# The first layer norm's sum is centred ahead of the last two parts of the output product, and the norm's steps are regrouped

## The chip, the cores and the metric

The kernel runs on one core of a Trainium2 chip. Its metric is the device time of one execution in microseconds (us); of several executions the median counts. A core has TensorE (PE in the profile, with PEld for its weight loads), VectorE (DVE), ScalarE (ACT), GpSimd (POOL) and SyncE (SP, which issues most of the transfers), each with a queue of its own that is worked off in order. They share the on-chip memory SBUF (128 partitions); PE writes its products to PSUM, from where DVE or ACT fetch them.

## The reference

One inference step of a decoder with two layers. 512 prompt positions and 8 x 8 sample positions, 576 columns in all, go through the same weights. The first layer has a mixer of two head groups, an RWKV-7 recurrence and a retention; their outputs are joined and multiplied by one output matrix. The second layer has a short convolution. Behind each mixer there is an MLP, and behind all four of them a layer norm over the 1024 features:

```python
def layer_norm(x, g, b):
    xf = x.astype(jnp.float32)
    mu = jnp.mean(xf, -1, keepdims=True)
    var = jnp.mean(jnp.square(xf - mu), -1, keepdims=True)
    return ((xf - mu) * lax.rsqrt(var + LN_EPS)).astype(x.dtype) * g + b
...
        x = layer_norm(ALPHA * x + y, ln1_g[l], ln1_b[l])
        x = layer_norm(ALPHA * x + sqrelu_mlp(x, w_up[l], w_down[l]), ln2_g[l], ln2_b[l])
```

with `y = concat([ya, yb]) @ w_out` in the first layer, and `sqrelu_mlp` the square of relu(x @ w_up), times w_down. The change is about the first of these norms, and about the order of the work ahead of it.

## The kernel before

Everything lies feature-major: a matrix of 1024 features by 576 columns is eight tiles of 128 x 576, and each tile is worked on in two halves of 288 columns, g=0 and g=1. A tile's statistics over the features are sums over partitions and tiles, which PE makes with a matrix of constants. Products of full accuracy are made in three matmuls: each operand is split into a high part `hi` (a cast on ACT, L77) and the rest `lo` (a subtraction on DVE, L78), and `mm3` multiplies hi by hi, lo by hi and hi by lo (L152, L153, L154).

*The mixer stage* ends at about 497 us. Twelve Python generators issue it: the input projection (`projs`), the preparation of the four head pairs of the recurrence (`pres`, `stages`, `back` 0 to 3 with the chained scans `ch` and the outputs `po`), the sample columns, the retention's front and back for four pairs, and `wout`, the output product. The function `drive` calls them in turn, and the order in which it does so, with the priority it sets, decides the order on the engines. Before the change `drive` reads this order from the table `SCHEDULE`, 424 pairs of a generator's number and a priority, worked out beforehand.

*The output product* (`Wout`) is added up in parts, as its inputs are finished (`WP`): part 0 multiplies the blocks k=0, 1, 2 of the joined heads, part 1 k=3, 4, 5, and part 2 k=6. Part 0 waits for recurrence pair 2 (`ya2`), part 1 for pair 3 (`ya3`) and the retention pairs 0 and 1, and part 2 for retention pair 2. For each of the eight output tiles m a part loads a piece of the weights (`wr`, two buffers), splits it on ACT (L1306) and POOL (L1307), multiplies into the PSUM tiles `wa`, and adds to x on DVE: L1336 in part 0, L1338 in parts 1 and 2. The weights for k=7 are loaded and split ahead of time (`keep`, after part 0). Their products (`acc<-hh,kh`) stand in the next stage, in front of the norm.

*The first norm* is fed one tile after the other by `ln_add`. On the first tile it makes an estimate of the mean from that tile alone (`cps`, L246), which seven subtractions on POOL and one on DVE take off all eight tiles (L255), so that squares stay small. Then each tile gets its last addition (L257), its sum `ps` (L283), its square on ACT (L260) and the square's sum `pq` (L283). `ln_finish` makes mean and variance, the reciprocal root by Ln and Exp on ACT with one Newton step on DVE (L294 to L302), and for each tile x - mean on DVE (L309), times the root on POOL or DVE (L310), and times gamma plus beta on ACT (L313). A split into hi and lo follows (L77, L78). All of it is done for g=0 and for g=1.

*The first MLP* begins with the head: four output tiles in ordinary products (`acc<-he`, `acc<-ho`), each with a Relu on ACT (L1588), a square on DVE (L1589, `evac_up`) and a split. Beside them POOL makes sums and differences of x (`ts`, L1564), which the products behind the head use (`acc<-ht`, function `gemm7`), in a scheme of seven products in place of eight. The second MLP, in the second layer, begins in the same way.

## Time and profile before

| quantity | value |
|---|---|
| time, median of 3 | 1573.41 us (1572.03 to 1576.05) |
| time of the profiled execution | 1570.47 us |
| its span | 1568.7 us |
| PE, DVE, ACT, POOL busy | 94%, 69%, 41%, 36% |
| last product of the input projection | 353.5 us |
| last x addition of part 0 | 437.6 us |
| last x addition of part 1 | 479.0 us |
| last x addition of part 2 | 497.0 us |
| first product of the first MLP | 523.1 us |
| first product behind its head | 571.5 us |

The span is the time from the first to the last recorded instruction; the profiled execution's own time is 1.8 us longer. All moments are counted from the span's start. In rows of the profile, `out<-in` names the tile that is written and those that are read, `x8` a count, and what stands behind `<-` in a group's last column is what ended the idle time ahead of it. A fp32 matmul that is not split leaves two records.

### The profile page before, as it was taken

To read this page: it belongs to the slowest core of one execution; us is meant where nothing else is said; L and a number is where in the kernel's file an instruction comes from. 1 tells how busy PE (TensorE), PEld (TensorE's weight loads), DVE (VectorE), ACT (ScalarE), POOL (GpSimd) and SP (SyncE) were. 2 spreads that over 40 slices of the span, in tenths; PEclk is the share of its full clock that TensorE was granted. 3 is DMA by queue.
4 is the path that set the end of the run, shared out by engine and by line. 5 is a ranking of instruction groups with operands and counts; after the bars stand their busy time and mean duration, and the time that the engine had idled before them with its cause. 6 is when DMAs were issued, how large, how long until landed. Compare 5 with 4: busy or idle time off the path is not lost.

```text
span 1568.7 us, 29898 instructions
## 1 busy us (share of the span) xinstructions
PE 1476.0 (94%) x11760; PEld 1421.9 (91%) x11760; DVE 1077.6 (69%) x2038; ACT 639.8 (41%) x1345; POOL 564.0 (36%) x643
## 2 busy tenths in 40 slices
PE   6999999998997889999999998989998999999995
PEld 6999898987886689999999997889988999999995
DVE  4656766675756795664846779899799575574755
ACT  4444334332233553342624545434365244251533
POOL 2032213336443551211302377555564121121355
PEclk9999999999898889999999999999999999999998
DMA  5333234435223013231322411223402314132221
GB/s 171 96 96 91 86 101 130 139 92 168 82 64 120 0 43 121 81 122 57 106 81 68 135 42 56 74 74 115 129 1 81 97 66 135 54 121 68 83 66 61
DMA packets 71197, 140.04 MB, mean 89 GB/s; under 512 B 21744, under 2 KB 31200, under 8 KB 71056
## 3 DMA queue, kind: packets, MB, share of 16 engines
q1 hardware_dynamic: 68224, 129.69, 26.6%
q0 software_dynamic: 1536, 5.57, 1.1%
q10 hardware_dynamic: 1296, 2.86, 0.6%
q8 instruction: 92, 1.51, 0.4%
q14 instruction: 49, 0.40, 0.1%
HBM read 124.39 MB, written 13.70 MB: 88 GB/s over the span
## 4 chain that ended last, share of the span: by engine, by line
PE 77%; DVE 11%; DMA 4%; POOL 4%; issue 3%; ACT 1%; SPq 1%; DVEq 0%; ACTq 0%; POOLq 0%
PE acc L152 21%; PE acc L153 21%; PE acc L154 21%; DVE wl L78 2%; PE mx L803 2%; DMA raw<-in_w 1%; DVE u L309 1%; POOL x L255 1%; DVE hl L78 1%; PE mx L700 1%; PE wa L152 1%; PE mx L542 1%; PE pq L283 1%; PE ps L283 1%; PE wa L154 1%
## 5 line engine op out<-in xcount | busy, mean ns | idle before, releaser
L77 ACT CAST wh<-raw 128x512 fp32r<-128x512 f32 x440 | 252.7, 618 | 411.2 <-PE acc L153 269.7
L78 DVE TENSOR_TENSOR wl<-raw,wh 128x512 fp32r<-128x512 f32 x440 | 330.2, 782 | 42.2 <-ACT wh L77 34.9
L153 PE MATMUL acc<-hl,wh 128*128 128x288 f32 x1180 | 349.0, 297 | 7.1 <-DVE hl L78 7.1
L154 PE MATMUL acc<-hh,wl 128*128 128x288 f32 x1180 | 348.6, 297 | 0.0
L152 PE MATMUL acc<-hh,wh 128*128 128x288 f32 x1180 | 344.4, 297 | 2.3 <-DVE ta L205 1.8
L153 PEld LDWEIGHTS acc<-hl,wh 128*128 128x128 f32 x1180 | 222.9, 189 | 8.0 <-DVE hl L78 7.5
L152 PEld LDWEIGHTS acc<-hh,wh 128*128 128x128 f32 x1180 | 221.2, 189 | 3.2 <-DVE ta L205 2.0
L154 PEld LDWEIGHTS acc<-hh,wl 128*128 128x128 f32 x1180 | 223.0, 189 | 0.3
L152 PE MATMUL acc<-xh,wh 128*128 128x288 f32 x480 | 148.3, 310 | 13.4 <-ACT xh L1395 12.4
L123 POOL TENSOR_TENSOR s<-raw 128x512 f32<-128x512 f32 x37 | 56.0, 1515 | 272.4 <-DMA raw<-in_w 206.1
L153 PE MATMUL acc<-xl,wh 128*128 128x288 f32 x480 | 146.2, 305 | 0.0
L154 PE MATMUL acc<-xh,wl 128*128 128x288 f32 x480 | 146.0, 304 | 0.0
L152 PE MATMUL acc<-ht,wh 128*128 128x288 f32 x444 | 130.9, 296 | 1.7 <-ACT wh L77 1.3
L153 PE MATMUL acc<-lt,wh 128*128 128x288 f32 x444 | 130.7, 295 | 0.0
L154 PE MATMUL acc<-ht,wl 128*128 128x288 f32 x444 | 130.5, 295 | 0.0
L123 POOL TENSOR_TENSOR raw<-raw 128x512 f32<-128x512 f32 x37 | 54.6, 1475 | 157.0 <-DVE raw L123 106.6
L152 PEld LDWEIGHTS acc<-xh,wh 128*128 128x128 f32 x480 | 91.5, 191 | 16.7 <-ACT xh L1395 12.8
L153 PE MATMUL acc<-lo,wh 128*128 128x288 f32 x352 | 105.2, 299 | 0.0
L152 PE MATMUL acc<-ho,wh 128*128 128x288 f32 x352 | 104.9, 300 | 0.1
L154 PE MATMUL acc<-ho,wl 128*128 128x288 f32 x352 | 104.9, 299 | 0.0
L153 PEld LDWEIGHTS acc<-xl,wh 128*128 128x128 f32 x480 | 91.5, 191 | 2.6 <-DVE xl L1396 0.7
L154 PEld LDWEIGHTS acc<-xh,wl 128*128 128x128 f32 x480 | 91.6, 191 | 1.5 <-issue 0.2
(461 smaller groups left out, 3498.0 us busy)
## 6 DMA issues: line engine op xcount, KB each, us to landing
raw<-in_w SPq DMA_DIRECT2D x160, 512.0 KB, 3.9
raw<-in_w SPq DMA_DIRECT2D x60, 256.0 KB, 2.9
A<-stg SPq DMA_DIRECT2D x9, 288.0 KB, 2.4
x<-in_x POOLq DMA_DIRECT2D x8, 288.0 KB, 7.4
out_y<-x SPq DMA_DIRECT2D x16, 144.0 KB, 1.8
wr<-in_w SPq DMA_DIRECT2D x16, 128.0 KB, 2.3
wr<-in_w SPq DMA_DIRECT2D x32, 64.0 KB, 2.0
kr<-A SPq DMA_DIRECT2D x6, 288.0 KB, 2.7
```

The source lines that it names most:

```text
L77: a = self.nc.scalar.copy(hi[:, s], src[:, s])
L78: b = self.nc.vector.tensor_tensor(out=lo[:, s], in0=src[:, s], in1=hi[:, s].bitcast(F32), op=ALU.subtract)
L123: tt = lambda e, o, x, y, op: e.tensor_tensor(out=o, in0=x, in1=y, op=op)
L152: nc.tensor.matmul(acc, lhsT=hi, rhs=xh, start=first, stop=False)
L153: nc.tensor.matmul(acc, lhsT=hi, rhs=xl, start=False, stop=False)
L154: nc.tensor.matmul(acc, lhsT=lo, rhs=xh, start=False, stop=last)
L255: e.tensor_tensor(out=t, in0=t, in1=c, op=ALU.subtract)
L283: self.nc.tensor.matmul(st[k], lhsT=self.ones1024, rhs=t, start=start, stop=stop)
L309: nc.vector.tensor_tensor(out=u, in0=r, in1=mn, op=ALU.subtract)
L542: self.nc.tensor.matmul(ps, lhsT=lhsT, rhs=rhs[:, o:o + n], start=True, stop=True)
L700: nc.tensor.matmul(both[h][:, i], lhsT=b3[q, c, h:h + 2].rearrange('p s t -> p (s t)'), rhs=la[q, c], start=True, stop=True)
L803: nc.tensor.matmul(ps[:, i], lhsT=bd(self.mb if n < 3 else self.Y0, j + i), rhs=v[:, j + i], start=True, stop=True)
```

## The change

Six things change.

1. *Centred weights.* For k=6 and k=7 the mean over the 1024 output features is taken off the weights, so that their products have no mean. `means` loads both blocks once more (four transfers of 256 KB into the not yet used tiles y6 and y7), adds them up on DVE, keeps the k=7 block, centred and split, in place of `keep`, and notes the two vectors; `weights` centres a k=6 piece on ACT. It loads k=6 for two output tiles at once.
2. *Centred sum.* Between parts 1 and 2 `center` makes the mean of x so far with 16 plain fp32 matmuls and takes it off in 16 subtractions on DVE. From there on x has no mean.
3. *The norm's steps.* `ln0_add` and `ln0_finish` replace `ln_add` and `ln_finish` for this norm: no first estimate, no sum, no mean. The squares of the first six tiles are added in pairs on POOL, so that five matmuls in place of 16 sum them up. The variance stays in PSUM, and the reciprocal root is made there. For each tile, DVE multiplies x by gamma and the root in one instruction, ACT adds beta for the hi part, DVE subtracts it for lo, and ACT adds beta once more for x itself.
4. *Squares of the MLP's head* (`evac_up`) go from DVE to ACT, in both MLPs.
5. *The order.* The table gives way to a planner: each generator has a clock, which a step moves on by its number in `RATE` times the step's size, and the one with the earliest clock among those that wait for nothing is called next.
6. `wout` issues `means` once the projection is done.

The table `SCHEDULE` is cut in the diff.

```diff
--- before.py
+++ after.py
@@ -281,6 +281,38 @@
         if start:
             st[k] = self.p_misc.tile([P, GN], F32, tag="misc", name='p' + n)
         self.nc.tensor.matmul(st[k], lhsT=self.ones1024, rhs=t, start=start, stop=stop)
+    def ln0_add(self, st, m, g, r, a):
+        nc = self.nc
+        st[g, m] = r
+        nc.vector.tensor_tensor(out=r, in0=r, in1=a, op=ALU.add)
+        t = self.p_tmp.tile([P, GN], F32, tag="t", name="lt", bufs=self.tb)
+        nc.scalar.activation(t, r, AF.Square)
+        if m >= 6: self.ln_mm(st, 'q', g, t, m == 7)
+        elif m % 2:
+            nc.gpsimd.tensor_tensor(out=t, in0=st[g, 'q'], in1=t, op=ALU.add)
+            self.ln_mm(st, 'q', g, t, False)
+        else: st[g, 'q'] = t
+    def ln0_finish(self, st, g, par, out):
+        nc, V = self.nc, self.nc.vector
+        pt, v = self.p_tmp, st[g, 'q', 'ps']
+        w0, w = [pt.tile([P, GN], F32, tag="t", name=n, bufs=self.tb) for n in ('w0', 'w')]
+        with self.tc.issue_after(self.pre.ins):
+            nc.scalar.activation(w0, v, AF.Ln, bias=self.eps)
+        nc.scalar.activation(w, w0, AF.Exp, scale=-0.5)
+        V.scalar_tensor_tensor(out=w0, in0=w, scalar=-0.5, in1=w, op0=ALU.mult, op1=ALU.mult)
+        V.scalar_tensor_tensor(out=v, in0=v, scalar=LN_EPS, in1=w0, op0=ALU.add, op1=ALU.mult)
+        V.scalar_tensor_tensor(out=v, in0=v, scalar=1.5, in1=w, op0=ALU.add, op1=ALU.mult)
+        gam, bet = par
+        for m in range(KT):
+            r, (hi, lo), b = st[g, m], out(m, g), bet[:, m:m + 1]
+            V.scalar_tensor_tensor(out=r, in0=r, scalar=gam[:, m:m + 1], in1=v, op0=ALU.mult, op1=ALU.mult)
+            x = nc.scalar.activation(hi, r, AF.Identity, bias=b)
+            y = V.scalar_tensor_tensor(out=lo, in0=r, scalar=b, in1=hi.bitcast(F32), op0=ALU.add, op1=ALU.subtract)
+            nc.scalar.activation(r, r, AF.Identity, bias=b)
+            if g and m == self.gated - 2: self.gate = [x.ins, y.ins]
     def ln_finish(self, st, g, par, out, last=False):
         nc = self.nc
@@ -1233,50 +1265,37 @@
             c(sh[1:][None]), c(wk(o['swkv'])), c(rt(o['sret'])), c(cv[1:][None]))
-SCHEDULE = (
-    (0, 100000), (1, 100000), (1, 100000), (2, 100000), (3, 100000), (4, 100000), (5, 100000), (6, 100000), (7, 100000), (8, 100000), (9, 100000),
...
-)
+RATE = (735.4, 69, 94, 102.8, 96.9, 129.4, 147, 133, 167.5, 137.3, 134, 148.1)
 def drive(tc, *gens):
-    base = tc.cur_priority
-    for c, p in SCHEDULE:
-        tc.cur_priority = base + p
-        next(gens[c], None)
-    tc.cur_priority = base + max(p for _, p in SCHEDULE) + 10000
+    base, n = tc.cur_priority, len(gens)
+    time, wait, live, held, now = [100000.0] * n, [None] * n, set(range(n)), set(), 100000.0
+    def free(c):
+        w = wait[c]
+        return w is None or (w() if callable(w) else w not in held)
+    while live:
+        ok = [c for c in live if free(c)]
+        c = min(ok, key=lambda c: (max(time[c], now) if wait[c] is not None else time[c], c))
+        if wait[c] is not None:
+            time[c] = max(time[c], now)
+            if not callable(wait[c]): held.add(wait[c])
+            wait[c] = None
+        now = max(now, time[c])
+        tc.cur_priority = base + int(time[c])
+        try:
+            y = next(gens[c])
+        except StopIteration:
+            live.discard(c)
+            continue
+        if callable(y): wait[c] = y
+        elif isinstance(y, tuple):
+            if y[0] > 0: wait[c] = y[1]
+            else: held.discard(y[1])
+        else: time[c] += RATE[c] * (1 if y is None else y)
+    tc.cur_priority = base + int(max(time)) + 10000
@@ -1296,19 +1315,58 @@
     def __init__(self, T, w):
         self.T, self.nc, self.w = T, T.nc, w
-        self.w7 = []
+        self.w7, self.less = [], {}
         self.y = [None] * 8
-    def weights(self, m, k0, n, keep=False):
-        t = self.wq.tile([P, 2 * P], F32, tag='wr', name='wr', bufs=2)[:, 0:n * P]
-        self.nc.sync.dma_start(t, self.w[30 + m, :, P * k0:P * (k0 + n)])
-        hi, lo = (self.wq.tile([P, n * P], F32R, name=f'k{c}{m}', bufs=1) if keep else self.wq.tile([P, 2 * P], F32R, tag=f'w{c}', name=c, bufs=2)[:, 0:n * P] for c in 'hl')
+    def weights(self, m, k0, n):
+        t = self.wq.tile([P, 2, P], F32, tag='wr', name='wr', bufs=2)
+        b = self.less.get(k0)
+        if b is None:
+            t = t[:, 0:n]
+            self.nc.sync.dma_start(t.rearrange('p m c -> p (m c)'), self.w[30 + m, :, P * k0:P * (k0 + n)])
+        else:
+            n = 2
+            self.nc.sync.dma_start(t, self.w[30 + m:32 + m, :, P * k0:P * (k0 + 1)].rearrange('m p c -> p m c'))
+            self.nc.scalar.activation(t, t, AF.Identity, bias=b)
+        hi, lo = (self.wq.tile([P, 2, P], F32R, tag=f'w{c}', name=c, bufs=2)[:, 0:n] for c in 'hl')
         self.nc.scalar.copy(hi, t)
         self.nc.gpsimd.tensor_tensor(out=lo, in0=t, in1=hi.bitcast(F32), op=ALU.subtract)
         return hi, lo
-    def keep(self):
-        self.w7 = [self.weights(m, 7, 1, True) for m in range(8)]
+    def means(self):
+        nc = self.nc
+        stage = [y[:, 0:512].rearrange('p (m c) -> p m c', m=4) for y in self.y[6:8]]
+        for k in (6, 7):
+            s = [self.wq.tile([P, 1], F32, name=f's{k}{h}', bufs=1) for h in range(2)]
+            for h, t in enumerate(stage):
+                nc.sync.dma_start(t, self.w[30 + 4 * h:34 + 4 * h, :, P * k:P * (k + 1)].rearrange('m p c -> p m c'))
+                nc.vector.tensor_reduce(out=s[h], in_=t, axis=AX.XY, op=ALU.add)
+            nc.vector.tensor_tensor(out=s[0], in0=s[0], in1=s[1], op=ALU.add)
+            nc.vector.tensor_scalar(out=s[0], in0=s[0], scalar1=-1.0 / 1024, scalar2=None, op0=ALU.mult)
+            self.less[k] = s[0]
+        for h, t in enumerate(stage):
+            hi, lo = (self.wq.tile([P, 4, P], F32R, name=f'k{c}{h}', bufs=1) for c in 'hl')
+            nc.scalar.activation(t, t, AF.Identity, bias=s[0])
+            nc.scalar.copy(hi, t)
+            nc.gpsimd.tensor_tensor(out=lo, in0=t, in1=hi.bitcast(F32), op=ALU.subtract)
+            self.w7 += [(hi[:, m], lo[:, m]) for m in range(4)]
+    def center(self, mx):
+        nc, T = self.nc, self.T
+        o = self.wq.tile([P, P], F32, name='wo', bufs=1)
+        nc.gpsimd.memset(o, 1 / 1024)
+        for g in range(2):
+            ps = mx.tile([P, 512], F32, tag='mx', name='mx')[:, 0:GN]
+            xs = [t[:, GN * g:GN * (g + 1)] for t in T.x]
+            for m, t in enumerate(xs):
+                nc.tensor.matmul(ps, lhsT=o, rhs=t, start=m == 0, stop=m == KT - 1)
+                if m % 2: yield 1
+            for t in xs: nc.vector.tensor_tensor(out=t, in0=t, in1=ps, op=ALU.subtract)
+            yield 3
     def part(self, ks, first):
         nc, T = self.nc, self.T
@@ -1326,10 +1384,12 @@
             accs = [self.acc.tile([P, GN], F32, tag='wa', name='wa') for _ in range(2)]
             for j in range(0, len(ks), 2):
                 n = min(2, len(ks) - j)
-                hi, lo = self.weights(m, ks[j], n)
+                if ks[j] not in self.less: hi, lo = self.weights(m, ks[j], n)
+                elif m % 2 == 0: two = self.weights(m, ks[j], n)
+                if ks[j] in self.less: hi, lo = (w[:, m % 2:m % 2 + 1] for w in two)
                 for g, a in enumerate(accs):
                     for x in range(n):
-                        T.mm3(a, hi[:, P * x:P * (x + 1)], lo[:, P * x:P * (x + 1)], *[c[:, GN * g:GN * (g + 1)] for c in h[ks[j + x]]], j + x == 0, j + x == len(ks) - 1)
+                        T.mm3(a, hi[:, x], lo[:, x], *[c[:, GN * g:GN * (g + 1)] for c in h[ks[j + x]]], j + x == 0, j + x == len(ks) - 1)
             for g, a in enumerate(accs):
                 r = T.x[m][:, GN * g:GN * (g + 1)]
                 if first:
@@ -1479,12 +1539,14 @@
                     yield from R.ret_back(p, *rt[p])
             def wout():
+                yield lambda: 'proj' in M.done
+                W.means()
                 for n, (ks, ns) in enumerate(WP):
                     for a in ns:
                         yield lambda a=a: a in M.done
                     W.y[0:6] = ['Y0', 'Y1'] + M.y[2:6]
                     yield from W.part(ks, n == 0)
-                    if n == 0: W.keep()
+                    if n == 1: yield from W.center(mxb)
             rt = {}
             W = Wout(T, i['w'])
             W.sp, W.stage = M.sp, lambda: M.e('stg')
@@ -1508,6 +1570,7 @@
             hp = pool('hp', 1, s2)
             T.ones1024 = hp.tile([P, P], F32, name='o1'); T.ones128 = hp.tile([P, P], F32, name='o2')
+            T.eps = hp.tile([P, 1], F32, name='ep'); nc.gpsimd.memset(T.eps, LN_EPS)
             nc.gpsimd.memset(T.ones1024, 1 / 1024); nc.gpsimd.memset(T.ones128, 1 / 128)
             pre = nc.scalar.preload_act_table_set('natural_log_exp_and_others')
             for a in M.tabled:
@@ -1586,7 +1649,7 @@
     def evac_up(m, g, a):
         t = tmp('rl'); nc.scalar.activation(t, a, AF.Relu)
-        nc.vector.tensor_tensor(out=t, in0=t, in1=t, op=ALU.mult)
+        nc.scalar.activation(t, t, AF.Square)
         split(cut(hs[m], gs[g]), t)
     def evac_up7(m):
@@ -1610,13 +1673,14 @@
                 T.gemm7(u + 16 * q + j, x7, evac_up7(j))
-    ev = res_evac(T.ln_state(0, x), lnpar(0), split_x, first=False)
+    st = T.ln_state(0, x)
     T.ensure(E0)
     for g in range(2):
         for m, (hi, lo) in enumerate(w7):
             a = T.p_acc.tile([P, GN], F32, tag='acc', name='acc')
             T.mm3(a, hi, lo, *hx(7, g), True, True)
-            ev(m, g, a)
+            T.ln0_add(st, m, g, x[m][:, gs[g]], a)
+        T.ln0_finish(st, g, lnpar(0), split_x)
     T.ensure(41)
     opened()
     xt += T.xt
```

The planner moves nearly all of the stage's later half. On PE, the place at which recurrence pair 3 is finished (`L542` before, `L574` now, the last products of `ya3`; `wa` are the output product's sums, `mx<-cst`, `rpo` and `mx<-rvt` belong to the retention). Before:

```order
L542 MATMUL mx<-gd,lw 128x288
L1131 MATMUL rpo<-rS,e 128x128
L542 MATMUL mx<-gd,lw 128x288
L969 MATMUL mx<-cst_170,hd 128x128 x4
L971 MATMUL mx<-cst_170,hd 128x64
L1160 MATMUL mx<-rvt,rkm 64x64 x16
L944 MATMUL mx<-cst_170,rot 64x128
L152 MATMUL wa<-hi_5490,h 128x288 x2
L1074 MATMUL mx<-cst_170,w_5345 128x128 x4
```

And now:

```order
L904 MATMUL po<-uv_127,lr_126 64x64 x16
L907 MATMUL po<-la_125 64x64 x14
L1001 MATMUL mx<-cst_170,hd 128x128 x4
L1003 MATMUL mx<-cst_170,hd 128x64
L524 MATMUL mx<-cst_170,hd 64x64 x18
L574 MATMUL mx<-gd,lw 128x288 x2
L152 MATMUL wa<-hi_5659,h 128x288 x2
L153 MATMUL wa<-lo_5660,h 128x288
L154 MATMUL wa<-hi_5659,l 128x288
```

Before, two retention pairs are still under way when pair 3 is finished, and their products stand among part 1 (`wa<-hi_5490`). Now the retention's last products stand in front of pair 3's, and behind these there is only part 1 (`wa<-hi_5659`) and what follows it.

On DVE, the norm for g=0. Before, with g=1's additions (L257) among it:

```order
L309 TENSOR_TENSOR u<-x_4552,ln 128x288
L300 TENSOR_TENSOR w_6299<-w 128x288
L255 TENSOR_TENSOR x_4548<-x_4548,ln 128x288
L257 TENSOR_TENSOR x_4549<-x_4549,acc 128x288
L301 SCALAR_TENSOR_TENSOR ln<-ln,w_6299 128x288
L257 TENSOR_TENSOR x_4550<-x_4550,acc 128x288
L302 SCALAR_TENSOR_TENSOR ln<-ln,w 128x288
L309 TENSOR_TENSOR u<-x_4553,ln 128x288
```

And now:

```order
L1398 TENSOR_TENSOR x_4262<-x_4262,wa 128x288 x2
L289 TENSOR_TENSOR x_4262<-x_4262,acc 128x288 x2
L305 SCALAR_TENSOR_TENSOR w_6269<-w 128x288
L306 SCALAR_TENSOR_TENSOR pq<-pq,w_6269 128x288
L307 SCALAR_TENSOR_TENSOR pq<-pq,w 128x288
L311 SCALAR_TENSOR_TENSOR x_4255<-x_4255,par,pq 128x288
```

Seven more products L311 follow, then the eight lo's L313. All additions to x, of both halves, now stand ahead of the norm's steps, and the subtraction of the mean is gone; the operand `pq` lies in PSUM, where `ln` lay in SBUF.

On ACT, the same place. Before:

```order
L260 ACTIVATE lt<-x_4555 128x288
L290 COPY ln<-ps 128x288
L292 ACTIVATE d<-ps 128x288
L297 ACTIVATE w_6299<-ln 128x288
L299 ACTIVATE w<-w_6299 128x288
L248 COPY ln<-cps 128x288
L313 ACTIVATE x_4548<-u,par 128x288
```

And now:

```order
L291 ACTIVATE lt<-x_4262 128x288
L303 ACTIVATE w_6269<-pq,ep 128x288
L304 ACTIVATE w<-w_6269 128x288
L291 ACTIVATE lt<-x_4255 128x288
L291 ACTIVATE lt<-x_4256 128x288
```

Six more squares (L291) of g=1 follow, and then g=0's eight hi parts (L312) and its affine steps (L314). So g=1's eight squares stand between g=0's Exp (L304) and its first hi part.

33 rows, old and new, of the table SCHEDULE are left out of this document.

## The prediction

> **What bounds the kernel now.** I read the two places that the change touches, and no others: the end of the mixer stage, and the first layer norm with the head of the first MLP behind it. First the page's busy times, its row of PE in 40 slices of 39.2 us, and the shares of the chain that ended last.
>
> ```profile
> PE 1476.0 (94%) x11760; PEld 1421.9 (91%) x11760; DVE 1077.6 (69%) x2038; ACT 639.8 (41%) x1345; POOL 564.0 (36%) x643
> PE   6999999998997889999999998989998999999995
> PE 77%; DVE 11%; DMA 4%; POOL 4%; issue 3%; ACT 1%; SPq 1%; DVEq 0%; ACTq 0%; POOLq 0%
> ```
>
> PE carries 77% of the chain; DVE and POOL carry 15%. The holes in PE's row are slices 10 to 14, from about 350 to 550 us. There I took a table of windows (busy time per engine, records in brackets, then PE's granted clock).
>
> ```profile
> 353.50:437.00 83.50, 74.91 (x818) 67.91 (x817) 51.47 (x132) 25.38 (x72) 42.97 (x59) 0.90 0.38 120
> 437.00:497.00 60.00, 49.61 (x402) 43.31 (x400) 40.07 (x101) 22.36 (x59) 23.25 (x40) 0.91 0.33 100
> 497.50:571.50 74.00, 60.64 (x312) 52.18 (x312) 55.09 (x86) 34.62 (x81) 41.18 (x42) 0.84 0.03 11
> 555.00:560.00 5.00, 3.07 (x24) 2.83 (x22) 5.00 (x5) 1.34 (x3) 5.00 (x6) 1.00 0.00 0
> 560.00:565.00 5.00, 2.21 (x9) 2.21 (x10) 5.00 (x7) 3.87 (x7) 3.39 (x4) 0.66 0.00 0
> ```
>
> In the mixer's tail PE is idle 19 of 143.5 us (83.50 - 74.91 + 60.00 - 49.61). In the 74 us from 497.5 on PE is idle 13.4; in the two rows of 5 us below that one DVE is busy throughout and PE idle 1.9 and 2.8: there DVE sets the pace. Three rows bracket that stage: the last addition of the output product, the first matmul of the MLP, and the first product of its odd tiles (gemm7).
>
> ```profile
> L1338 DVE TENSOR_TENSOR x<-x,wa x32: 441/448/456, 449.3 to 497.0; 128x288 f32<-128x288 f32 x32
> L152 PE MATMUL acc<-he,wh x176: 289/295/855, 523.1 to 1488.3; 128*128 128x288 f32 x176
> L152 PE MATMUL acc<-ht,wh x444: 289/295/413, 571.5 to 1497.8; 128*128 128x288 f32 x148
> ```
>
> I call the norm's start Z, now 497.5. The MLP starts at Z+26, gemm7 at Z+74. The waits from 497 to 580 say for whom (total, times, longest):
>
> ```profile
> POOL u L310 <- DVE ln L302: 15.0, 1, 15.0
> ACT x L313 <- DVE u L310: 11.9, 5, 5.2
> POOL x L255 <- ACT ln L248: 7.9, 1, 7.9
> PE acc L153 <- DVE hl L78: 7.1, 2, 4.7
> ACT hh L77 <- DVE rl L1589: 6.0, 2, 4.2
> ```
>
> All are elementwise work that comes late: the norm's subtractions and multiplications first, then the hi/lo splits that stand behind them on DVE.
>
> **The change part by part.** The norm first. The groups from 497 to 575 (busy us, mean ns, then idle before):
>
> ```profile
> L283 PE MATMUL ps<-x,o 128*128 128x288 f32 x32 | 13.6, 520 | 5.8 <-DVE x L257 3.7 <-DVE x L255 2.0
> L309 DVE TENSOR_TENSOR u<-x,ln 128x288 f32<-128x288 f32 x16 | 9.5, 640 | 0.0
> L313 ACT ACTIVATE x<-u,par 128x288 f32<-128x288 f32 x16 | 9.5, 621 | 11.9 <-DVE u L310 11.9
> L260 ACT ACTIVATE lt<-x 128x288 f32<-128x288 f32 x16 | 6.9, 440 | 4.3 <-DVE x L257 3.8 <-DVE x L255 0.5
> L257 DVE TENSOR_TENSOR x<-x,acc 128x288 f32<-128x288 f32 x14 | 6.2, 449 | 4.4 <-POOL x L255 4.4
> L310 DVE TENSOR_TENSOR u<-u,ln 128x288 f32<-128x288 f32 x6 | 5.8, 988 | 0.0
> L1589 DVE TENSOR_TENSOR rl<-rl 128x288 f32<-128x288 f32 x7 | 5.6, 796 | 0.0
> L78 DVE TENSOR_TENSOR lo<-x,ho 128x288 fp32r<-128x288 f32 x8 | 5.7, 709 | 1.4 <-ACT ho L77 1.4
> L1564 POOL TENSOR_TENSOR ts<-x,ts 128x288 f32<-128x288 f32 x8 | 8.9, 1132 | 0.0
> L1588 ACT ACTIVATE rl<-acc 128x288 f32<-128x288 f32 x8 | 3.1, 406 | 0.0
> L77 ACT CAST hh<-rl 128x288 fp32r<-128x288 f32 x6 | 2.5, 445 | 6.0 <-DVE rl L1589 6.0
> L78 DVE TENSOR_TENSOR lt<-ts,ht 128x576 fp32r<-128x576 f32 x8 | 5.6, 746 | 0.0
> L77 ACT CAST ht<-ts 128x576 fp32r<-128x576 f32 x8 | 4.9, 669 | 0.0
> ```
>
> *Up to the first MLP matmul.* Gone are the centring round (cps, its copy, 16 subtractions on POOL and DVE), the 16 sums `ps` and 6 of 16 squares' matmuls. What is left behind the last addition is one chain: square 0.44, one matmul 0.5, Ln and Exp 0.44 each, three DVE steps and a product 4 x 0.45, the hi activation 0.5: 4.1 us. The order adds a queue: ACT takes g=1's eight squares (8 x 0.44 = 3.5) between Exp and the first hi, against 1.8 on DVE meanwhile, so 1.7 more, and I assume 0.3 us for each of seven hand-overs between engines, 2.1. The MLP starts at Z+8 instead of Z+26.
>
> *Up to gemm7.* Four engines could set its start. PE: the head's 192 matmuls (four tiles, two halves, eight k, three products) at the run's mean of 0.126 us (1476.0 / 11760) are 24, so Z+32. ACT: 8 squares 3.5, four Ln/Exp 1.8, 16 hi and 16 affine activations between L260's and L313's price, 14.1 to 19.9, and 10.3 of Relus, squares and casts (8 x (0.406 + 0.44 + 0.445)): 30 to 36, from Z+1.5, so Z+31 to Z+37; behind its last affine come POOL's last four sums `ts` (4 x 1.1) and their split (0.75 on DVE, 0.67 on ACT): Z+37 to Z+43. DVE: of its 55.1 it loses L309, L310, L257 and L1589, 27.1; it gains 16 products in L311 at 0.449, 7.2; and 16 lo's in L313, at 0.45 to 0.99 each, replace 16 splits at the 0.709 of the `lo` row, -4.1 to +4.5: 31 to 40, from Z+2.5, so Z+34 to Z+42. I take Z+42, at the upper ends, since the engines also wait for each other. The gain is 74 - 42 = 32, with ends 42 (PE's Z+32) and 19 (rival 2).
>
> This rests on one thing in L311: its second operand stands in PSUM. L257, also with an operand in PSUM, took 449 ns beside a busy POOL, while L309 and L310 with both in SBUF took 640 and 988. The Trainium skill (SBUF — State Buffer, Who interferes with whom) says that a VectorE instruction with two SBUF inputs contends with GpSimd's reads, and one with at most one does not; these rows agree. By that rule the lo's (L313, two SBUF inputs) pay whenever POOL's sums run: half of the 16 at 0.99 instead of 0.45 would be 4.3 us more on DVE, which would speak for the late end that I chose.
>
> *The squares of evac_up* go from DVE (0.796) to ACT (0.44): eight in this head, counted above, and eight in the second MLP's head, which I put at 0 with ends -2 and +2, as there the old norm stays and DVE stays its bound.
>
> *The mixer stage.* The order is no longer the table but a planner's, so everything between 353 and 497 moves. What the change adds of work: 16 fp32 matmuls for the mean (in the chain one such matmul, of two records, takes 0.48: 7.7 us), 16 subtractions on DVE (at L257's 0.449, 7.2), 9 of the 16 last-part products that now stand in the norm (9 x 3 x 0.126 = 3.4), and four reductions over 128x512 that the trace lacks (between DVE's 0.78 for L78 of that size and POOL's 1.5 for L123; I take 0.8, and nothing of it shows, since it lies behind the projection's end among 19 idle us of PE; uncovered it is 3 to 6). Removed: the eight casts and subtractions of `keep`. As part 2's weights come in pairs there are 4 loads instead of 8. The nearest rows:
>
> ```profile
> 508.15 0.48 PE ps L283 x2
> L78 DVE TENSOR_TENSOR wl<-raw,wh 128x512 fp32r<-128x512 f32 x440 | 330.2, 782 | 42.2 <-ACT wh L77 34.9
> L123 POOL TENSOR_TENSOR s<-raw 128x512 f32<-128x512 f32 x37 | 56.0, 1515 | 272.4 <-DMA raw<-in_w 206.1
> L1306 ACT CAST h<-wr x40: 282/299/407, 356.2 to 492.7; 128x128 fp32r<-128x128 f32 x24, 128x256 fp32r<-128x256 f32 x16
> L1307 POOL TENSOR_TENSOR l<-wr,h x40: 443/462/960, 361.2 to 493.0; 128x128 fp32r<-128x128 f32 x24, 128x256 fp32r<-128x256 f32 x16
> wr<-in_w SPq DMA_DIRECT2D x16, 128.0 KB, 2.3
> L872 PE MATMUL po<-uv,lr x128: 222/222/270, 180.7 to 418.9; 128*64 128x64 f32 x128
> L542 PE MATMUL mx<-gd,lw x4: 406/406/408, 436.3 to 437.2; 128*128 128x288 f32 x4
> L154 PE MATMUL acc<-xh,wl x59: 290/295/442, 300.5 to 353.5; 128*128 128x288 f32 x59
> ```
>
> Where Z falls I bound by two routes. By count: between the projection's last product and the norm PE has 814 instructions now (353.5 to 497, 0.176 each) and 971 afterwards, and the projection's end moves 114 instructions up, to about 340. At today's 0.176 Z is 510; at the 0.126 of a full PE it would be 461, which the waits forbid. By the chain: weights bound each of part 1's eight tiles to 2.3 (load) + 0.3 + 0.46 and a wait, 3.5 us, and the order puts all of part 1 behind `ya3`. Part 0 runs from wkv pair 2's end (405 by the count) to 433; from `po` to `ya3`'s products it was 18 us (418.9 to 436.3), so `ya3` is there at 452; part 1 to 480, then the mean's last matmuls, 16 products and what is left of k=7: 20 to 500. I take 502.5, so +5, with ends -10 (half of the 19 idle us recovered) and +25 (next part). The 16 subtractions stand between parts 1 and 2 on DVE; the next additions and hence PE's `wa` buffers wait for them, but the order puts six products of k=7 (6 x 3 x 0.126 = 2.3 us) and two tiles of part 2 there, so of 7.2 some 3 show, within these 20.
>
> The sum against the profiled execution's own 1570.5: +5 - 32 + 0 = -27, 1543.5. That run lay 2.9 below the median of the runs shown (1573.4), so on their footing **1546 us**.
>
> **The rivals.** (1) *Serial tail, the slower side.* PE's queue reaches part 1 only behind `ya3`, which now stands behind both retention groups. If one step of pair 3's chain of scans is late, all parts behind it shift. For it: those scans took 29 us among part 0 (28 `ch` products, two a step), and now share DVE with two retentions. Against it: their rows lie among part 0's still, with other work between them.
>
> ```profile
> L863 PE MATMUL ch<-la x28: 218/267/366, 389.7 to 418.5; 64*64 64x64 f32 x28
> ```
>
> From Z = 529.5 (497.5 + 32) on the norm's gain is spent; at 536 the time is 1573.4 + 38.5 - 32 = 1580. (2) *Half the gain.* ACT's hi, DVE's lo, PE's product and ACT's Relu make a ring, and ACT's queue holds Relus ahead of later hi's. If the waits of today's rows for `hl` (7.1) and for `rl` (6.0) stay, gemm7 starts at Z+55 (42 + 13): 19 gained, 5 lost, 1559. For it: ACT's sum comes within 6 us of DVE's, where today ACT is busy only 34.6 of 74; against it, L1589, which ended one of these waits, leaves DVE. (3) *Short tail.* The planner recovers idle time, Z = 488, and the norm gives 34: 1573.4 - 9.5 - 34 = 1530. For it: 19 us idle; against it, 11 us of work that came forward. (4) *Centring does not free the head:* the first weights of the MLP (raw) come late, since part 2 used to cover their load. The chain shows such a load at 486.06:
>
> ```profile
> 486.06 5.53 DMA raw<-in_w
> ```
>
> The loads now stand among part 1's on SP, so they are issued earlier; they would have to come two such loads late, 11 us, to give 1557. I count this with (2).
>
> **How the numbers follow.** The forecast has 0.50, (1) 0.17, (2) with (4) 0.18, (3) 0.15. The likeliest case's own range joins +5 (8 less, 10 more) and -32 (10 less, 13 more) as independent, 1533 to 1562. Down to (3)'s 1525 (0.07 beyond it) and up into (1), 1575 (0.13 beyond it), it holds 8 in 10: 1525 to 1575. One measurement tells apart about 0.3%, 5 us, so same is 1568.7 to 1578.1. Faster: all of the forecast, (2) and (3), less the upper edge, 0.78; same: the part of (1) where Z lies near 529 and that edge, 0.09; slower, Z beyond 534: 0.13.
>
> **What would show it.** In the changed profile: first `acc<-he` at about 8 us behind the last x addition, first `acc<-ht` at 42; no PE wait for `hl` of 4 us; L311 near 0.45, L313 0.45 to 1; DVE not full from Z+15 on. The last x addition at 500 to 505; if it is past 525, (1) holds. If gemm7 starts past Z+50, with ACT full, (2). A PE wait for raw or `wh` at the head shows (4). Wrong altogether would be: the norm shorter and the MLP behind it longer by as much.

## The result, and the profile after

| | before | after |
|---|---|---|
| time, median of 4 each, taken together | 1572.72 us (1571.64 to 1576.05) | 1594.35 us (1590.21 to 1595.44) |
| time of the profiled execution | 1570.47 us | 1595.17 us |
| its span | 1568.7 us | 1593.4 us |
| last x addition starts | 497.0 us | 550.9 us |
| first product of the first MLP | 523.1 us | 561.1 us |
| first product behind its head (gemm7) | 571.5 us | 590.0 us |
| from there to the end of the span | 997.2 us | 1003.4 us |

The change makes the kernel slower: the ratio of after to before is 1.0129 (95% interval 1.0105 to 1.0154), some 20 us more, where 27 less were forecast. The spans differ by 24.7 us, and the table divides this: the mixer stage ends 53.9 later, the stretch from there to gemm7 is 35.4 shorter (39.1 in place of 74.5), and what follows is 6.2 longer: 53.9 - 35.4 + 6.2 = 24.7.

From the page of the changed kernel, PE's busy tenths and its granted clock in 40 slices of 39.8 us, and the shares of the chain that ended last:

```profile
PE   6999999997897799999999998999998999999996
PEclk9999999977797999999999998999999999999998
PE 74%; DVE 12%; DMA 4%; issue 4%; POOL 3%; ACT 2%; SPq 1%; ACTq 0%; DVEq 0%; POOLq 0%
```

Slices 10 to 14 of PE (the first is 1) read 7 8 9 7 7, against 8 9 9 7 8 before, and the clock is at 7 tenths in four of the slices from 9 to 13. The holes are deeper, and they are in the mixer stage. Behind them, where the norm and the head stand now, PE reads 9.

**The mixer stage.** First the chained scan of recurrence pair 2 (`ch`, 14 plain fp32 matmuls; the prediction's 28 products are their records), and the products that finish this pair, before. The columns are the count, the least, median and greatest duration in ns, and the first and last moment.

```profile
L863 PE MATMUL ch<-la x28: 218/267/366, 311.8 to 330.3; 64*64 64x64 f32 x28
L542 PE MATMUL mx<-gd,lw x4: 404/404/405, 350.3 to 351.1; 128*128 128x288 f32 x4
```

The same after, and then, in the order of time, the additions of part 0, the products that finish pair 3 (`ya3`), the subtractions of the centring, and the additions of parts 1 and 2, which share a row:

```profile
L895 PE MATMUL ch<-la x28: 218/246/366, 382.0 to 404.1; 64*64 64x64 f32 x28
L574 PE MATMUL mx<-gd,lw x4: 687/687/687, 435.3 to 436.7; 128*128 128x288 f32 x4
L1396 DVE SCALAR_TENSOR_TENSOR x<-x,wa x16: 439/453/456, 442.9 to 473.4; 128x288 f32<-128x288 f32 x16
L574 PE MATMUL mx<-gd,lw x4: 687/687/849, 489.6 to 491.2; 128*128 128x288 f32 x4
L1368 DVE TENSOR_TENSOR x<-x,mx x16: 447/449/455, 530.0 to 535.5; 128x288 f32<-128x288 f32 x16
L1398 DVE TENSOR_TENSOR x<-x,wa x32: 442/449/455, 498.2 to 550.9; 128x288 f32<-128x288 f32 x32
```

Before, pair 2's scan ran beside the input projection and was over when that ended, at 353.5. Now it starts at 382.0, behind the projection's end, which has hardly moved (356.1), and the pair is finished 85 us later (435.3 against 350.3). Part 0 needs this pair, and starts 6 us behind it. Pair 3 (`ya3`) comes at 489.6 instead of 436.3, part 1 at 498.2 instead of 449.3. In places the stage has become one chain of steps. Two windows of the changed kernel show how little lies beside it there, and a third is the head of the MLP, for below (length, busy time and records of PE, PEld, DVE, ACT and POOL, PE's granted clock, the share of the DMA engines, GB/s):

```profile
360.00:380.00 20.00, 12.14 (x115) 10.54 (x116) 10.77 (x30) 4.21 (x10) 8.48 (x12) 0.58 0.85 263
480.00:494.00 14.00, 6.15 (x47) 4.22 (x47) 7.37 (x22) 3.48 (x7) 0.94 (x2) 0.59 0.02 5
561.10:590.00 28.90, 28.90 (x218) 28.85 (x217) 28.80 (x42) 25.69 (x61) 17.07 (x16) 1.00 0.06 20
```

From 480 to 494 no engine is busy for more than 7.4 of 14 us: pair 3's last steps run alone. Who waits for whom in the stage is in the waits of DVE and PE (total, times, longest), two rows from 320 to 445, then two from 445 to 551:

```profile
DVE s L1346 <- DMA y<-in_w: 19.1, 2, 11.8
PE rpo L1163 <- DVE rS L1156: 7.9, 1, 7.9
PE mx L524 <- DVE hd L1038: 5.0, 1, 5.0
DVE x L1398 <- PE wa L154: 23.6, 8, 6.1
```

The first is new and belongs to the change: the sums over the weights wait for their load on DVE's queue.

**The norm and the head.** The third window above is the head of the MLP, from its first product to gemm7's: PE is never idle in it. The two rows that bound it:

```profile
L152 PE MATMUL acc<-he,wh x176: 291/293/510, 561.1 to 1512.4; 128*128 128x288 f32 x176
L152 PE MATMUL acc<-ht,wh x444: 290/294/445, 590.0 to 1521.9; 128*128 128x288 f32 x148
```

With the norm's start Z now at 551.4, the MLP starts at Z+9.7 and gemm7 at Z+38.6.

### The profile page after: what moved, and what is told of

Read it like the earlier page. It is cut to its first block, busy times and chain, and to the rows that moved or that the text cites. A ratio compares the mean times of both kernels' runs of the same rounds, so it can differ in the third digit from the quotient of the medians.

```text
span 1593.4 us, 29836 instructions
## 1 busy us (share of the span) xinstructions
PE 1491.0 (94%) x11744; PEld 1435.2 (90%) x11744; DVE 1070.6 (67%) x2036; ACT 646.1 (41%) x1351; POOL 547.8 (34%) x617
## 4 chain that ended last, share of the span: by engine, by line
PE 74%; DVE 12%; DMA 4%; issue 4%; POOL 3%; ACT 2%; SPq 1%; ACTq 0%; DVEq 0%; POOLq 0%
PE acc L152 20%; PE acc L153 20%; PE acc L154 20%; DVE wl L78 3%; PE mx L835 2%; DMA raw<-in_w 1%; DVE u L341 1%; DVE hl L78 1%; PE wa L152 1%; PE wa L154 1%; PE mx L732 1%; PE wa L153 1%; DMA y<-in_w 1%; SPq L814 1%; DMA wr<-in_w 1%
## 5 line engine op out<-in xcount | busy, mean ns | idle before, releaser
L152 PE MATMUL acc<-xh,wh 128*128 128x288 f32 x480 | 150.7, 315 | 15.3 <-ACT xh L1455 12.1
## 6 DMA issues: line engine op xcount, KB each, us to landing
out_y<-x SPq DMA_DIRECT2D x16, 144.0 KB, 1.8
```

What stands on the lines that cost most here:

```text
L152: nc.tensor.matmul(acc, lhsT=hi, rhs=xh, start=first, stop=False)
```

## The experiments

Two theories on the 54 us at first. **A, the order:** the planner puts the recurrence's steps later than the table did, whatever else is changed. **B, the weights' sums:** the wait of 19.1 us above, on DVE's queue, holds up the retention and the recurrence behind it. The experiments with the planner start from the changed kernel or the one before; those "with the table" from e2. Between experiments it is the ratios that are compared, each to the kernel before as it ran beside that experiment: its median was 1571.78 us beside e1 to e4, 1573.54 beside e5 to e8 and 1576.18 beside e9 to e11.

**e1. The planner alone.** The kernel before, with the old norm and uncentred weights, ordered by the planner:

```diff
-SCHEDULE = ( ... )
+RATE = (735.4, 69, 94, 102.8, 96.9, 129.4, 147, 133, 167.5, 137.3, 134, 148.1)
 def drive(tc, *gens):
-    for c, p in SCHEDULE:
...
+    while live:
...
```

> The kernel before, with the planner in place of the table and nothing else. Theory A (the planner's order is what made the mixer stage longer): the last x addition of part 2 moves from 497 to 525 to 545, and since the old norm stays, the time is 1600 to 1620 us. Theory B (the loads and sums of the weights' means, for which DVE waited 19 us in the changed kernel, made it longer, and the order did not): the last x addition stays at 497 to 505 and the time is 1573 to 1581.

Measured: 1604.09 us, ratio 1.0208 (1.0184 to 1.0233), 32 us slower than the kernel before. Its additions of parts 1 and 2, and the first product of gemm7:

```profile
L1325 DVE TENSOR_TENSOR x<-x,wa x32: 441/453/455, 494.4 to 536.1; 128x288 f32<-128x288 f32 x32
L152 PE MATMUL acc<-ht,wh x444: 289/295/403, 609.3 to 1536.0; 128*128 128x288 f32 x148
```

The last addition stands at 536.1, 39.1 later than before, with none of the centring in the program. gemm7 comes at Z+72.7, near the old norm's Z+74 in the kernel before. This profiled execution took 1609.4 us, 5 above the median of its four, so its 39.1 may be a few us too many.

**e2. Everything but the planner.** The changed kernel, ordered by the table, with one entry added for `means` and ten for `center`:

```diff
-RATE = (735.4, 69, ...)
+SCHEDULE = ( ... )
 def drive(tc, *gens):
+    for c, p in SCHEDULE:
+        tc.cur_priority = base + p
+        next(gens[c], None)
...
```

> The changed kernel with the table of the kernel before in place of the planner; the generator of the output product gets one more entry for the weights' means and ten for the centring, the others keep theirs. Theory A: the last x addition at 500 to 512 (11 us of added PE work among 19 us of idle time), the norm's and head's gain of 35 us stays, the time is 1545 to 1560. Theory B: the last x addition at 525 to 545 and the time is 1575 to 1592.

Measured: 1550.74 us, ratio 0.9869 (0.9848 to 0.9891), 21 us faster than before and 44 faster than the change. From its profile:

```profile
L895 PE MATMUL ch<-la x28: 218/267/292, 312.1 to 330.3; 64*64 64x64 f32 x28
L1437 DVE TENSOR_TENSOR x<-x,wa x32: 433/453/455, 444.9 to 503.1; 128x288 f32<-128x288 f32 x32
L152 PE MATMUL acc<-he,wh x176: 291/293/813, 517.4 to 1468.9; 128*128 128x288 f32 x176
L152 PE MATMUL acc<-ht,wh x444: 290/294/445, 546.7 to 1478.4; 128*128 128x288 f32 x148
445.00:480.00 35.00, 35.00 (x305) 31.16 (x304) 18.58 (x50) 10.62 (x31) 12.13 (x19) 1.00 0.22 69
```

Pair 2's scan is back beside the projection. The last addition is at 503.1, 6.1 later than before, with all of the centring in it: the 16 matmuls of the mean start between 446.6 and 479.4, where PE is busy throughout at the full clock. So A holds, by e1 and e2 from both sides. This version is faster than the kernel before and the changed one, and no other run is clearly better.

**e3. The planner without the weights' sums.** The changed kernel, with the loads of k=6 and the four sums left out, the means set to zero:

```diff
-            for h, t in enumerate(stage):
-                nc.sync.dma_start(t, self.w[30 + 4 * h:34 + 4 * h, ...])
-                nc.vector.tensor_reduce(out=s[h], in_=t, axis=AX.XY, op=ALU.add)
...
+            nc.gpsimd.memset(s[0], 0.0)
             self.less[k] = s[0]
+        for h, t in enumerate(stage):
+            nc.sync.dma_start(t, self.w[30 + 4 * h:34 + 4 * h, :, P * 7:P * 8].rearrange('m p c -> p m c'))
```

> The changed kernel, planner included, without the sums of the weights: the means are zeros, the two loads of k=6 and the four reductions with them are left out, so that the weights of k=6 and k=7 are not centred; all other work stays. Theory A: DVE's wait of 19 us goes, but the parts still stand behind the late recurrence pairs: 1583 to 1592. Theory B: the last x addition falls to 510 to 525 and the time to 1555 to 1572.

Measured: 1590.11 us, ratio 1.0109 (1.0085 to 1.0134); the last addition is at 547.8 instead of 550.9. By the last addition 3 us of the 54 come from the sums, by the medians 4 us of the time, and the intervals of the two ratios overlap. B falls as the main cause: DVE's 19.1 us go, and in the same stretch it then waits 15.3 us for PE (L1171), so DVE was not the bottleneck there.

**e4. The head's squares back on DVE.**

```diff
-        nc.scalar.activation(t, t, AF.Square)
+        nc.vector.tensor_tensor(out=t, in0=t, in1=t, op=ALU.mult)
```

> The changed kernel with the squares of both MLP heads on DVE again. It prices the sixteen squares alone. If DVE is what the head and the first tiles of gemm7 wait for (PE waited 4.6 us for the lt splits there), eight squares of 0.8 us come back onto it and the time is 3 to 7 us above the changed kernel's 1594, most of it ahead of the first acc<-ht; if ACT is the bound, it is 3 to 6 below it. The mixer stage stays as it is in both theories.

Measured: 1594.37 us, ratio 1.0142 (1.0117 to 1.0168), against 1594.35 with the squares on ACT: no difference. gemm7 starts at 589.0, that is Z+38.7, as in the change (Z+38.6), although five of the squares (4.6 us) now stand on DVE ahead of it.

**e5 and e6. Three numbers of RATE.** If it is the order, what in it? The table's entries tell the pace at which each generator was called. For nine generators this is their number in `RATE`; for recurrence pairs 2 and 3 (`RATE[5]`, `RATE[6]`) and the retention's fronts (`RATE[8]`) it is half of it. Pair 2's first step, four units long, moves its clock on by 259 in the table (from 114086 to 114345) and by 4 x 129.4 = 518 in the planner. So the planner calls these three half as often as the table did. e5 halves the three numbers in the changed kernel, e6 only pair 2's:

```diff
-RATE = (735.4, 69, 94, 102.8, 96.9, 129.4, 147, 133, 167.5, 137.3, 134, 148.1)
+RATE = (735.4, 69, 94, 102.8, 96.9, 64.7, 73.5, 133, 83.75, 137.3, 134, 148.1)
```

> The changed kernel with three of the planner's twelve numbers halved: those of recurrence pairs 2 and 3 (129.4 to 64.7 and 147 to 73.5) and of the retention's fronts (167.5 to 83.75). In the table of the kernel before, the steps of these three generators stand at just these halves (pair 2's first step of 4 moved its clock by 259, the planner's moves it by 518). Theory A1 (these three numbers place the recurrence too late, and the planner as such does no harm): pair 2's chained scan is back among the projection (310 to 340 instead of 382 to 404), the last x addition of part 2 at 498 to 510, and the time 1545 to 1560, as with the table. Theory A2 (the planner's locks and waits cost by themselves): the scan stays late and the time is above 1575.

> The changed kernel with only recurrence pair 2's number halved (129.4 to 64.7). If pair 2's late scan alone holds part 0 up, its scan comes forward by 40 us or more, part 0 starts at 390 to 400 instead of 443, and the time is 1550 to 1570. If pair 3 and the retention's fronts, still at their slow numbers, decide the end (the serial tail behind ya3), part 0 starts earlier but parts 1 and 2 do not: the last x addition stays above 530 and the time above 1575.

Measured: e5 1564.5 us, ratio 0.9941 (0.9921 to 0.9961); e6 1571.9 us, ratio 0.9991 (0.9976 to 1.0007). The scan of pair 2, the additions of parts 1 and 2, and in e5 the projection's last products:

```profile
L895 PE MATMUL ch<-la x28: 218/267/366, 324.2 to 352.3; 64*64 64x64 f32 x28
L1398 DVE TENSOR_TENSOR x<-x,wa x32: 439/448/456, 465.7 to 522.3; 128x288 f32<-128x288 f32 x32
L152 PE MATMUL acc<-xh,wh x60: 292/295/607, 299.7 to 375.0; 128*128 128x288 f32 x60
```

And in e6:

```profile
L895 PE MATMUL ch<-la x28: 218/218/267, 322.3 to 343.0; 64*64 64x64 f32 x28
L1398 DVE TENSOR_TENSOR x<-x,wa x32: 443/451/458, 473.0 to 527.1; 128x288 f32<-128x288 f32 x32
```

One number takes back 22 us, three take back 30 of the 44 that lie between the change and e2: pair 2's scan returns to the projection, and the last addition comes to 527.1 and 522.3. The other 14 us remain. Neither theory of e5 holds as it stands: the scan comes back, as A1 says, but the time lies between A1's 1560 and A2's 1575. In e6 part 0 starts at 398.7, as the first theory says, and the time is 2 us above its range. In e5 the projection ends at 375.3 instead of 356.1, so what is gained for the pairs seems in part to be paid there. Which of the planner's other differences from the table (its locks, its waits) makes this up wasn't tried, and stays open.

**e7. The table without the weights' sums**, e3's edit on e2.

> The changed kernel with the table, and without the sums of the weights: means of zero, the two loads of k=6 and the four reductions left out, so that these weights are not centred. It bounds what the sums cost when the order is the table's: DVE waited 10.6 us for their loads there. If that wait shows in the end, the time is 1538 to 1546 against the 1550.7 with them; if it is covered, as 19 us of it nearly were with the planner (4 us shown), it is 1547 to 1552.

Measured: 1551.6 us, ratio 0.9865 (0.9845 to 0.9885): the same as with the sums (0.9869). With the table they cost nothing that these runs can tell.

**e8. The sums on ACT** instead of DVE, on e2 (the new line's first argument, a conditional that always gives `t`, is written as `t` here):

```diff
-                nc.vector.tensor_reduce(out=s[h], in_=t, axis=AX.XY, op=ALU.add)
+                nc.scalar.activation(t, t, AF.Identity, accum_out=s[h])
```

> The changed kernel with the table, the four sums of the weights made on ACT (an identity that also adds up, in place) instead of DVE, so that ACT waits for the four loads and DVE does not. Nothing is left out. If DVE's wait of 10.6 us costs time, it is 1540 to 1548; if ACT's queue, which also carries the retention's copies, holds PE up as much, it stays at 1549 to 1554.

Measured: 1554.35 us, ratio 0.9883 (0.986 to 0.9906), nothing gained. The wait goes along; from the waits of e2 and of e8:

```profile
DVE s L1385 <- DMA y<-in_w: 10.6, 3, 5.0
```

```profile
ACT y L1385 <- DMA y<-in_w: 10.1, 2, 8.0
```

**e9. All squares summed by PE**, without POOL's sums of pairs, on e2:

```diff
-        if m >= 6: self.ln_mm(st, 'q', g, t, m == 7)
-        elif m % 2:
-            nc.gpsimd.tensor_tensor(out=t, in0=st[g, 'q'], in1=t, op=ALU.add)
-            self.ln_mm(st, 'q', g, t, False)
-        else: st[g, 'q'] = t
+        self.ln_mm(st, 'q', g, t, m == 7)
```

> The changed kernel with the table, all eight squares of a half summed up by PE itself: POOL's three additions of pairs are gone, three more plain matmuls per half come instead (6 x 0.48 = 2.9 us of PE). In the kernel with the table PE waited 4.6 us for those additions ahead of the norm, and the first acc<-he came 13.7 us after the last x addition of part 2, against 8 forecast. If the pairs are what is late, first acc<-he comes 2 to 4 us earlier and the time is 1546 to 1549; if PE's added work eats it, or the chain of additions on DVE is what ends last, it stays at 1550 to 1553.

Measured: 1554.83 us, ratio 0.988 (0.9859 to 0.9901). In the profile the wait for the pair sums is gone (in e2 4.6 us, in after 2.7; 1.5 us for ACT's squares stand in its place), and the MLP starts at 514.0 instead of 517.4, gemm7 at 543.8 instead of 546.7, as the first case says. The profiled execution was the fastest of its four (1548.55); by the median the time can't be told from e2's. The wait in e2, and in after:

```profile
PE pq L283 <- POOL lt L294: 4.6, 3, 2.7
```

```profile
PE pq L283 <- POOL lt L294: 2.7, 1, 2.7
```

**e10. The reciprocal root in SBUF**, so that the product L311 has both of its tiles there, on e2:

```diff
-        V.scalar_tensor_tensor(out=v, in0=v, scalar=1.5, in1=w, op0=ALU.add, op1=ALU.mult)
+        z = pt.tile([P, GN], F32, tag="t", name='vs', bufs=self.tb)
+        V.scalar_tensor_tensor(out=z, in0=v, scalar=1.5, in1=w, op0=ALU.add, op1=ALU.mult)
+        v = z
```

> The changed kernel with the table, the norm's reciprocal root written to SBUF by its last Newton step, so that L311 reads x and the root both from SBUF; nothing else. The prediction said the norm's gain rests on the root lying in PSUM. If so, L311 goes from 0.51 us to 0.64 to 1.0 and the time up by 2 to 8 us, to 1553 to 1559. If POOL has nothing to read at that time (its sums waited 14 us for ACT's affine steps there), L311 stays at 0.45 to 0.52 and the time at 1549 to 1552.

Measured: 1553.79 us, ratio 0.987 (0.9854 to 0.9886), no difference from e2's ratio. The products in after (in PSUM), and in e10 (in SBUF, line 313 there):

```profile
L311 DVE SCALAR_TENSOR_TENSOR x<-x,par,pq x16: 509/510/515, 556.8 to 568.1; 128x288 f32<-128x288 f32 x16
```

```profile
L313 DVE SCALAR_TENSOR_TENSOR x<-x,par,vs x16: 505/513/1522, 511.6 to 527.3; 128x288 f32<-128x288 f32 x16
```

The medians are the same, but they hide one half: the mean is 675 ns in e10 and 508 in e2, and one of the 16 takes 1.52 us. Which products are slow, and why, is in the next section.

**e11. The centring later.** In e2, the entries of `center` get a priority behind the retention's last ones (132300 in place of 129227).

> The changed kernel with the table, the ten entries of the centring at a later priority (132300 instead of 129375, that is, behind the last retention pair's steps where the order allows it). With the table the 16 subtractions filled DVE from 479 to 486 ahead of that pair's norm, and its output came at 495.6 instead of 483.7. If this delay is what holds part 2 up, the pair comes 3 to 8 us earlier and the time is 1543 to 1548; if part 2's additions need the subtractions just as much, it is 1549 to 1555.

Measured: 1552.37 us, ratio 0.9862 (0.9844 to 0.988), no difference; part 2's last addition is at 503.6 (503.1 in e2). But the edit hardly moved what it was to move: the subtractions start between 480.3 and 486.9 (479.4 and 485.5 in e2), most of them still ahead of the pair's norm, and the pair's output (L1198) comes at 495.7 for 495.6. So whether they hold part 2 up stays untested.

## Why the prediction was wrong

**The step that failed is "Where Z falls".** It put Z at 502.5, +5, with ends -10 and +25; it was 551.4, +53.9. Both routes rest on a count of instructions at today's mean pace. *By count*, Z was to be 510, from three terms: the projection's end 13.5 us earlier (340), 971 instructions behind it for 814 (28 us at 0.176 each), and the same pace. The trace has records, to a few per cent, and two for a plain fp32 matmul. From the projection's last product to Z there are, before, after and in e2:

```profile
353.50:497.50 144.00, 124.54 (x1219) 111.25 (x1217) 91.96 (x233) 47.73 (x129) 66.22 (x98) 0.90 0.36 112
356.10:551.40 195.30, 159.69 (x1504) 139.85 (x1503) 118.92 (x308) 55.30 (x142) 72.54 (x97) 0.82 0.31 94
353.00:503.60 150.60, 136.69 (x1265) 119.96 (x1263) 102.54 (x257) 48.08 (x126) 67.24 (x92) 0.90 0.32 101
```

The end of the projection came 2.6 us later, not 13.5 earlier. Behind it PE makes 285 records more, 33.7 us at the pace before (144.0 / 1219 = 0.118 each). In e2, with the same new work, there are only 46 more, so most of the 285 come from the order. And the pace is 0.130, which is 17.6 us more (in e2 it is 0.119). These three make the 53.9. Beside the forecast's terms, of the 41 us between 510 and 551 the pace has some 18, the projection's end 16 and the count the rest. The projection is the surprise: the pairs' work was taken out from beside it, and yet it ended no earlier. Its last 16 us, before and after:

```profile
340.00:356.10 16.10, 16.10 (x166) 14.89 (x165) 7.29 (x21) 4.43 (x13) 4.74 (x10) 1.00 0.35 86
340.00:356.10 16.10, 16.10 (x74) 12.43 (x74) 1.29 (x2) 0.92 (x4) 3.56 (x5) 0.58 0.04 3
```

By its records PE is busy throughout in both, but it makes 166 of them at a granted clock of 1.00 before, and 74 at 0.58 after. From 343 to 352 the new order also sets a small fp32 product (`mx<-la,s`) behind each of the projection's, which then start 0.86 us apart (but for one longer gap); from 352.7 on, where they stand alone, it is 0.24. How much is the clock and how much the order wasn't separated.

*By the chain*, Z was to be 500. Pair 2 was to be there at 405, by the count, and part 0 to start then; its first addition came at 442.9, 38 us late. `ya3` was put at 452, 19 behind part 0's end (433); it came at 489.6, 16 behind it (473.4), so this link held. Part 1 was to take 28 us from there and took 40 to the first subtraction (530.0); the rest, 20, took 21. So 38 of the 51 us that this route missed come from its start, which the count had set, and 12 from part 1. How slow such a chain is shows from 480 to 494: PE makes 47 records in 14 us, 0.298 each, where each step waits for DVE, ACT or PE.

I counted the steps that the planner moved and followed only pair 3's. The rival "Serial tail" had the right mechanism and too small a price: it let one step of pair 3 be late, by 32 to 38.5, for 1573 to 1580. Two pairs were late: before, pair 2's scan lay beside the projection; now the two scans follow one another behind it (382.0 to 404.1 and 446.8 to 466.8). Adding up: the planner alone is +39 (e1), and with it the rest of the stage's new work another 15, of which the sums are 3 (547.8 against 550.9); with the table the same work is +6.1 in all. The +5 of the forecast is thus what the centring costs in an order that is left as it was.

**The norm, -32.** Right, at -35.4: gemm7 at Z+38.6 for 42, the MLP at Z+9.7 for 8. With the table (e2) it is -30.9 (gemm7 at Z+43.1, the MLP at Z+13.8; the pair sums on POOL hold PE up for 4.6). That it is so near is in part luck, as the step erred on who sets it. I had put PE at Z+32, and ACT and DVE at up to Z+43. In after PE is busy 28.90 of the head's 28.90 us, with 218 records at 0.133: my 192 at the run's mean of 0.126 had the count and the pace too low, 24 for 29. DVE, at 28.80, is as full, but it doesn't set gemm7's start: in e4, with 4.6 us of squares back on it, it is as full (29.00 of 29.10 us) and gemm7 comes at the same Z+38.7, since DVE then makes fewer of the later weights' splits in that time (two `wl` for six). ACT (25.69) doesn't set it either. Neither the ring of rival 2 nor a late weight (rival 4) shows.

**Given back, +6.2, not in the forecast.** The 25 us behind gemm7's start, before and after:

```profile
571.50:596.50 25.00, 23.65 (x177) 23.42 (x178) 24.23 (x43) 16.93 (x35) 7.47 (x6) 1.00 0.48 152
590.00:615.00 25.00, 21.28 (x148) 20.99 (x147) 23.59 (x38) 14.63 (x30) 10.90 (x8) 0.93 0.44 126
```

PE makes 29 records fewer, 3.9 us at 23.65 / 177. It waits for the lo part of POOL's sums (two waits from 551 to 615, and the group of the splits: busy, mean ns, idle before):

```profile
POOL ts L1627 <- ACT x L314: 14.6, 1, 14.6
PE acc L153 <- DVE lt L78: 3.7, 1, 3.7
L78 DVE TENSOR_TENSOR lt<-ts,ht 128x576 fp32r<-128x576 f32 x8 | 7.7, 978 | 0.0
```

gemm7 needs those sums, POOL starts them only when ACT has added beta to x (L314), behind all the hi parts, and DVE then splits them at 978 ns each (746 before). The step that named POOL's last four sums and their split as the end of ACT's row was right on the place; what it missed is that gemm7 can start on the first of them and then stand still. e2 shows the same 6.0, and from gemm7 to the end the eleven runs with the regrouped norm take 1001.7 to 1006.4 us, the two with the old one 997.2 and 998.0 (e1); so it belongs to the regrouped norm and not to the order. Why the last 2 us come isn't known. With the table the forecast's terms would read +6.1 - 30.9 + 6.0 = -18.8, the difference of the spans (1549.9 - 1568.7).

**The squares, 0.** Right by e4.

**"This rests on one thing in L311: its second operand stands in PSUM."** The mechanism is right, but little rests on it. In e10, with both operands in SBUF, g=0's eight products run beside POOL and g=1's do not. The products in these two stretches (length, DVE's time on them and their count, PE's clock, the DMA), and POOL's work, which has no more until 531:

```profile
511.50:517.70 6.20, 6.08 (x8) 0.50 0.23 78
524.30:527.80 3.50, 3.50 (x8) 1.00 0.00 0
511.90 1.36 POOL L123 TENSOR_TENSOR s<-raw 128x512 f32<-128x512 f32 x1 [7.47 <-DMA raw<-in_w]
513.22 2.94 POOL L294 TENSOR_TENSOR lt<-lt 128x288 f32<-128x288 f32 x3
```

Eight products take 6.08 us beside POOL and 3.50 without it. In e2, with the root in PSUM, the first of them also run beside POOL (until 514.7), and none is longer than 0.515:

```profile
L311 DVE SCALAR_TENSOR_TENSOR x<-x,par,pq x16: 505/508/515, 513.1 to 524.4; 128x288 f32<-128x288 f32 x16
```

So the operand in PSUM saves DVE 2.6 us in that order, and the time doesn't show them. In after the products run from 556.8, and POOL is at work only until 558.3; then its `ts` wait 14.6 us for ACT, until 572.9. The rule of the Trainium skill (SBUF — State Buffer, Who interferes with whom) speaks of instructions that overlap, and the rows of e10 agree with it, as does the place in after where the lo parts and POOL's sums begin to overlap. Three rows of that timeline (start, length, the idle time ahead and what ended it): the lo parts, with two inputs in SBUF, double from 0.52 to 1.08 as POOL starts.

```profile
572.63 0.52 DVE L313 SCALAR_TENSOR_TENSOR hl<-x,par,hh 128x288 fp32r<-128x288 f32 x1
572.92 0.89 POOL L1627 TENSOR_TENSOR ts<-x 128x288 f32<-128x288 f32 x1 [14.63 <-ACT x L314]
573.06 1.08 DVE L313 SCALAR_TENSOR_TENSOR lo<-x,par,ho 128x288 fp32r<-128x288 f32 x1
```

**The loads and sums of `means`,** "nothing of it shows": with the table so (e7), with the planner some 3 to 4 us (e3).

## What to carry to other kernels

A count of instructions at the mean pace of a stage says when a full engine is done; it says nothing on a chain of short steps that wait for each other, so where a change moves such a chain out from beside a long full stretch, follow it step by step and take its whole length as the price until something is shown to lie beside it. Nor does the stretch that it leaves get shorter by the chain's share: here the projection ended no earlier. An order that is generated anew belongs in an experiment of its own, apart from the work that is ordered: here the work gained 21 us with the old order, and the new order took 44. When a planner replaces a table, compare the paces that it works with against those that the table shows, one by one: one number at twice its value was worth 22 us.

## What the runs showed of the hardware

The thin stage seems to have cost twice, as PE's granted clock fell with it: 0.59 from 480 to 494, and the products that finish a pair took 687 ns where they took 404 before, a ratio of 0.588. The Trainium skill (TensorE: Matmul & The Clock Gate, What's actually happening) says that the clock is halved until the engine has been busy for some microseconds; the trace agrees in kind. It was not expected that a PE whose records fill the time can stay slow. In e1, from 415 to 435:

```profile
415.00:435.00 20.00, 19.38 (x191) 17.09 (x191) 8.39 (x27) 3.45 (x8) 5.95 (x8) 0.50 0.01 2
```

PE is busy 19.38 of 20 us there at a granted clock of 0.50, with 191 records of small products, and the end of the projection in after (340 to 356.1, above) is of the same kind, at 0.58. Taken at their word, these rows do not fit that rule. But the ends of matmuls are modelled in the trace, so the busy time may be too long, and what keeps the clock down there was not tried.
